# A float32 encoder trunk on one core: two matmuls of 512 and 256 columns per weight tile, in place of three of 256

## The chip, the cores and the metric

The kernel runs on one core of one Trainium2 chip. The metric is device time of one execution in microseconds, as the median of the runs. Before the change it was 1114.94 us (three runs, 1114.20 to 1115.59).

## The reference, cut to what matters

Two layers work on 256 tokens of 1024 channels in float32. All that the change touches are dense products and what follows directly on them:

```python
def swiglu(h, w_gate, w_up, w_down):              # 1024 -> 2816 -> 1024
    return (jax.nn.silu(h @ w_gate) * (h @ w_up)) @ w_down
...
x = x + 0.5 * swiglu(rmsnorm(x, g_ffa[i]), ...)   # SwiGLU a
...                                               # mixer: attention and a long convolution
y = jnp.concatenate([_rms(y_na), _rms(y_hy)], axis=-1) * g_out[i]
x = x + y @ w_out[i]                              # output projection
x = x + 0.5 * swiglu(rmsnorm(x, g_ffb[i]), ...)   # SwiGLU b
x = x + jax.nn.sigmoid(rmsnorm(x, g_ple[i]) @ w_ple_gate[i]) * (p[i] @ w_ple_proj[i])
```

After two such layers comes a last RMS norm.

## The kernel before

Activations lie with channels on the 128 partitions and the 256 tokens side by side, so a block of 128 channels is a tile of 128x256. To keep float32 accuracy on a TensorE that multiplies shorter numbers, every operand is split in two: a rounded high part and the remainder. A product of a 128x128 weight tile with a block of activations is `mm3`, three matmuls of 256 columns into one accumulator: weight high with activation high (L165), weight high with activation low (L166), weight low with activation high (L167). The two parts of an activation lie side by side in one tile of 512 columns (`xg`, `act`, `y`).

Weights stream from memory in float32. For every 8 weight tiles ScalarE (ACT) rounds them to the high part `wh` (the cast on L250, 128x1024) and VectorE (DVE) subtracts that to get the low part `wl` (L253); in the mixer every third of these subtractions goes to GpSimd (POOL). Six such halves can wait in buffers for TensorE.

What sets the order: TensorE and ACT execute in the order in which the Python code emits; DVE, POOL and SyncE execute in an order that a scheduler fixed when the program was built. Emission is paced by the products. After every third product (`TICK = 3`) a tick lets each live "fiber" (a generator of the smaller work) go one step, up to its next `yield`. An instruction that waits on DVE holds up what stands behind it on DVE.

The stages of a layer, in order: SwiGLU a (44 gate and up products of 8 weight tiles, then 8 down blocks of 22 tiles), the mixer, the output projection (8 blocks, 4 tiles of attention and 4 of convolution each), SwiGLU b as SwiGLU a, and the gated per-layer input (8 gate products of 8 tiles). The mixer's column products, scores and transforms keep `mm3` in both versions.

- In the SwiGLU a pair of gate and up shares one PSUM bank (128x512). DVE multiplies both by `rb`, the reciprocal root mean square of each token (L439; for the first two pairs L436 and L437, 256 columns each), ACT takes silu (L442), DVE multiplies silu and up (L445), ACT rounds it (L447), DVE subtracts (L449). The first four products, called heads below, run side by side over the eight input blocks `xg`, since these come one by one from the stage before.
- Normalisation is late: `Rstd` sums the squares, TensorE reduces them (L379), DVE does Newton's steps for the root (L387, L352 to L361), DVE and ACT put the result on a diagonal (L391 to L397), and TensorE spreads it (L403, L404). Squares are taken on ACT (L314) and added on POOL (L317).
- In the projection each block's two sums are multiplied by `rna` or `rhy` on DVE (L886) and added to `x`, the first on POOL, the second on DVE (both L887). When `x` of a block is final, ACT makes the high part (L329) and DVE the low part (L331) of `xg`, the next stage's input; on DVE this is one instruction.
- In the gate of the per-layer input DVE multiplies by `rb` (L985), ACT takes the sigmoid (L988), DVE multiplies (L992) and adds to `x` (L993); then follows the next stage's `xg`, or, at the very end, the transposition (L1009) and the last norm.

Of the kernel before, what the change touches and what calls it, by code (L numbers as in the profile page):

```python
# [28 lines left out]
HALF = 8  # L29

# [29 lines left out]
# columns of the packed per-partition parameters of one layer  # L60
# [15 lines left out]
def hybrid_trunk(ctx: ExitStack, tc: tile.TileContext, w, xT, pT, rpb, small, wf, zT, dft, idft, decay, out):  # L76
# [42 lines left out]
    class Fiber:  # L119
        """Work of several engines, emitted step by step between the products."""  # L120
# [39 lines left out]
    def rest(n):  # L160
        for _ in range(n):
            yield

    def mm3(o, lh, ll, rh, rl, start, stop):
        PE.matmul(o, lh, rh, start=start, stop=False)  # L165
        PE.matmul(o, lh, rl, start=False, stop=False)  # L166
        PE.matmul(o, ll, rh, start=False, stop=stop)  # L167
        if not Pace.inside:
            Pace.total += 1
            Pace.count += o.free_size() // T if hasattr(o, "free_size") else o.shape[-1] // T  # L170
            while Pace.count >= TICK:
                Pace.count -= TICK
                tick()

# [21 lines left out]
    # even times, odd times, and the latter's negative; real and imaginary parts  # L196
# [37 lines left out]
    def part(steps=1):  # L234
        """The next 8 weight tiles in their two 12-bit parts."""
        n = Stream.parted
        Stream.parted += 1
        while Stream.loaded < min(n // 2 + 2, DEPTH * PIECES):
            load()
        raw = Stream.raws[n // 2]  # L240
        h = whp.tile([P, HALF, P], F32R, tag="wh", name=nm("wh"))
        l = wlp.tile([P, HALF, P], F32R, tag="wl", name=nm("wl"))
        fb = Fiber(None)
        Stream.ready[n] = (h, l, fb)

        def go():
            k = HALF // steps
            for a in range(0, HALF, k):
                src = raw[:, n % 2 * HALF + a : n % 2 * HALF + a + k]
                S.copy(h[:, a : a + k], src)  # L250
                yield
                e = G if Stream.on_pool and n % Stream.on_pool == 0 else V
                e.tensor_sub(l[:, a : a + k], src, f(h[:, a : a + k]))  # L253
# [39 lines left out]
    class Inputs:  # L293
        """The two parts of g * x of the norm at hand."""
# [5 lines left out]
        def __getitem__(self, c):  # L300
            hl, fb = self.xs[c]
            fb.finish()
            return hl[:, :T], hl[:, T:]

    class Squares:
        """Sum of the squares of `n` blocks, in whatever order they come."""
# [27 lines left out]
    def onward(i, cg, c, before):  # L334
        """After `before`, which brings x[c] up to date, the next norm's input."""
        hl = t2(F32R, "xg")

        def go():
            yield from before
            yield  # L340
            yield from prep(i, cg, c, hl)

        scaled.append((hl, spawn(go())))

    def rsqrt(v):
        """v ** -0.5 of two columns by Newton's steps from the exponent's halving."""
# [18 lines left out]
    class Rstd:  # L365
        """1/rms of each token: `r`, tokens on partitions, and `dst`, on all partitions."""
# [58 lines left out]
    def ffn(i, cg_next, i_next):  # L425
# [5 lines left out]
        def gated(pg, pu, joint, hl):  # L431
            yield from rest(EV)
            yield from rs.wait()
            gu = t2(s="gu")
            if joint is None:
                V.tensor_mul(gu[:, :T], pg, rb)  # L436
                V.tensor_mul(gu[:, T:], pu, rb)  # L437
            else:
                V.tensor_tensor(v2(gu), v2(joint), rb2(), op=ALU.mult)  # L439
            yield  # L440
            s = t1()
            S.activation(s, gu[:, :T], AF.Silu)  # L442
            yield
            a = t1()
            V.tensor_mul(a, s, gu[:, T:])  # L445
            yield
            S.copy(hl[:, :T], a)  # L447
            yield
            V.tensor_sub(hl[:, T:], a, f(hl[:, :T]))  # L449

        def start(*a):
            hl = t2(F32R, "act")
            act.append((hl, spawn(gated(*a, hl))))

        heads = [bank()[:, :T] for _ in range(4)]
        for c in range(KD):
            xh, xl = xs[c]
            for o in heads:
                wh, wl = ws.next()
                mm3(o, wh, wl, xh, xl, c == 0, c == KD - 1)  # L460
        for j in (0, 2):
            start(heads[j], heads[j + 1], None)
        for ff in range(2, NF):
            b = bank()
            for o in (b[:, :T], b[:, T:]):
                product(o, ws, xs)
            start(None, None, b)
        ws = Tiles()
        new_norm()
        for c in range(KD):  # L470
            ps = bank()[:, :T]
            for k in range(NF):
                wh, wl = ws.next()
                hl, fb = act[k]
                fb.finish()
                mm3(ps, wh, wl, hl[:, :T], hl[:, T:], k == 0, k == NF - 1)

            def half_step(c=c, ps=ps):
                yield from rest(EV)
                V.scalar_tensor_tensor(x[c], ps, 0.5, x[c], op0=ALU.mult, op1=ALU.add)  # L480

            onward(i_next, cg_next, c, half_step())
# [8 lines left out]
    def filter_steps(i):  # L491
# [96 lines left out]
        # sums and differences of the even and the odd times' spectra  # L588
# [22 lines left out]
    def mixer(i):  # L611
# [3 lines left out]
        def columns(between=None):  # L615
            """Two blocks of 128 columns of u from the next 16 weight tiles."""
# [7 lines left out]
        # values, tokens on partitions  # L624
# [36 lines left out]
        class QK:  # L661
            """Queries and keys of a pair of heads, the queries with zeros for the other head."""
# [25 lines left out]
        class Head:  # L688
            """One head's probabilities: the scores' softmax, then turned over."""
# [56 lines left out]
        def head_norm(src, sq, ch, hl):  # L746
            """The two parts of g * y, and its squares added up."""
# [21 lines left out]
        def conv(b, chans, res):  # L769
            """Short convolution of the two blocks of channels in a bank."""  # L770
# [66 lines left out]
        def spectral(a, ps):  # L837
            """The gated input's spectrum, frequencies on partitions, times the filter's."""
# [34 lines left out]
        def project(wo, c, parts):  # L873
            ps = bank()[:, :T]
            for k in range(4):
# [3 lines left out]
                mm3(ps, wh, wl, hl[:, :T], hl[:, T:], k == 0, k == 3)  # L879
            return ps  # L880

        def add(c, ps, st, e):
            yield from rest(EV)
            yield from st.wait()
            t = t1()
            V.tensor_mul(t, ps, st.dst)  # L886
# [71 lines left out]
    def ple(i, last, given):  # L958
# [22 lines left out]
        def update(c, ps):  # L981
            yield from rest(PLE_EV)
            yield from rs.wait()
            g = t1()
            V.tensor_mul(g, ps, rb)  # L985
# [27 lines left out]
        for c in range(KD):  # L1013
            ps = bank()[:, :T]
            product(ps, ws, xs)
# [80 lines left out]
def _rpb_index():  # L1096
    """Where the bias of (token of the query, token of the key) lies; the last place outside the window."""
# [7 lines left out]
def _tiles(wm):  # L1105
    """[K, M] -> [M tiles, K tiles, 128, 128]."""
# [4 lines left out]
def _weights(a):  # L1111
# [9 lines left out]
    def swiglu(i, s):  # L1121
# [4 lines left out]
        put(_tiles(a[f"w_ff{s}_down"][i]))  # L1126
# [77 lines left out]
```

## Time and profile before

| | before |
|---|---|
| median of three runs | 1114.94 us |
| span of the profiled execution (first to last instruction) | 1112.9 us |
| granted TensorE clock, mean | 0.996 |
| PE matmuls | 8828 |
| DMA queues, share of 16 engines | 49% |

The profiled execution spans 1112.9 us, and about 2 us of the median lie around it. In the rows of a timeline the columns are start, duration, engine, line, operation, output and inputs, count; what stands in brackets is idle time before it and what ended it. A matmul's duration contains its way through the array, so the distance from one start to the next is what a matmul costs. On DVE too, back-to-back instructions overlap by some 0.08 us.

### The profile page before, as it was taken

To read this page: it belongs to the slowest core of one execution; us is meant where nothing else is said; L and a number is where in the kernel's file an instruction comes from. 1 tells how busy PE (TensorE), PEld (TensorE's weight loads), DVE (VectorE), ACT (ScalarE), POOL (GpSimd) and SP (SyncE) were. 2 spreads that over 40 slices of the span, in tenths; PEclk is the share of its full clock that TensorE was granted. 3 is DMA by queue.
4 is the path that set the end of the run, shared out by engine and by line. 5 is a ranking of instruction groups with operands and counts; after the bars stand their busy time and mean duration, and the time that the engine had idled before them with its cause. 6 is when DMAs were issued, how large, how long until landed. Compare 5 with 4: busy or idle time off the path is not lost.

```text
span 1112.9 us, 21462 instructions
## 1 busy us (share of the span) xinstructions
PE 1087.2 (98%) x8828; PEld 1074.4 (97%) x8828; DVE 840.5 (76%) x1352; ACT 600.3 (54%) x1006; POOL 205.1 (18%) x182
## 2 busy tenths in 40 slices
PE   7999999999999999999999999999999999999996
PEld 7999999999999999999999999999989999999995
DVE  4988777798999766655878878677899986665554
ACT  6555455376746444444655455544855554444444
POOL 3000111544362000011100002125433700000111
PEclk9999999999999999999999999999999999999998
DMA  8565455454335555455455554454523464555421
GB/s 319 215 236 201 154 191 186 170 173 169 114 117 197 190 189 190 176 175 183 161 195 200 215 188 174 173 185 152 190 77 114 142 217 183 189 189 186 176 95 39
DMA packets 32994, 194.29 MB, mean 175 GB/s; under 512 B 3584, under 2 KB 6528, under 8 KB 10880
## 3 DMA queue, kind: packets, MB, share of 16 engines
q1 hardware_dynamic: 32896, 192.92, 48.4%
q8 instruction: 69, 1.13, 0.4%
q14 instruction: 29, 0.24, 0.1%
HBM read 191.86 MB, written 1.05 MB: 173 GB/s over the span
## 4 chain that ended last, share of the span: by engine, by line
PE 80%; DVE 11%; ACT 4%; issue 3%; DMA 1%; POOL 1%; SPq 0%; ACTq 0%; DVEq 0%; POOLq 0%
PE ps L166 26%; PE ps L167 26%; PE ps L165 26%; DVE wl L253 2%; ACT wh L250 2%; DMA raw<-in_w 1%; DVE rt L360 1%; DVE s L783 1%; DVE s L886 1%; DVE x L887 1%; ACT t L723 1%; DVE xg L331 0%; POOL acc L317 0%; ACT t L716 0%; DVE y L752 0%
## 5 line engine op out<-in xcount | busy, mean ns | idle before, releaser
L253 DVE TENSOR_TENSOR wl<-raw,wh 128x1024 fp32r<-128x1024 f32 (+1 forms) x328 | 410.9, 1257 | 193.7 <-ACT wh L250 191.7
L250 ACT CAST wh<-raw 128x1024 fp32r<-128x1024 f32 (+1 forms) x350 | 362.0, 1040 | 321.6 <-PE ps L166 226.8
L165 PE MATMUL ps<-xg,wh 128*128 128x256 f32 x1856 | 528.2, 285 | 5.9 <-ACT xg L1032 5.9
L166 PE MATMUL ps<-xg,wh 128*128 128x256 f32 x1856 | 527.5, 284 | 5.4 <-DVE xg L331 5.3
L167 PE MATMUL ps<-xg,wl 128*128 128x256 f32 x1856 | 526.9, 284 | 0.0
L166 PEld LDWEIGHTS ps<-xg,wh 128*128 128x128 f32 x1856 | 357.7, 193 | 7.2 <-DVE xg L331 6.3
L165 PEld LDWEIGHTS ps<-xg,wh 128*128 128x128 f32 x1856 | 357.8, 193 | 6.3 <-ACT xg L1032 5.9
L167 PEld LDWEIGHTS ps<-xg,wl 128*128 128x128 f32 x1856 | 357.7, 193 | 0.0
L167 PE MATMUL ps<-act,wl 128*128 128x256 f32 x704 | 199.4, 283 | 0.0
L165 PE MATMUL ps<-act,wh 128*128 128x256 f32 x704 | 199.4, 283 | 0.0
L166 PE MATMUL ps<-act,wh 128*128 128x256 f32 x704 | 199.4, 283 | 0.0
L317 POOL TENSOR_TENSOR acc<-acc,q 128x256 f32<-128x256 f32 x62 | 65.9, 1064 | 541.2 <-ACT q L314 524.8
L165 PEld LDWEIGHTS ps<-act,wh 128*128 128x128 f32 x704 | 135.2, 192 | 0.4
L166 PEld LDWEIGHTS ps<-act,wh 128*128 128x128 f32 x704 | 135.2, 192 | 0.4
L167 PEld LDWEIGHTS ps<-act,wl 128*128 128x128 f32 x704 | 135.2, 192 | 0.0
L439 DVE TENSOR_TENSOR gu<-ps,rb 128x512 f32<-128x512 f32 x80 | 55.0, 689 | 20.6 <-PE ps L167 19.0
L253 POOL TENSOR_TENSOR wl<-raw,wh 128x1024 fp32r<-128x1024 f32 x22 | 55.0, 2499 | 62.7 <-ACT wh L250 49.9
L566 POOL TENSOR_TENSOR t<-t,t 128x512 f32<-128x512 f32 x4 | 5.7, 1414 | 225.7 <-PE ps L167 121.0
L329 ACT ACTIVATE xg<-x,sm 128x256 fp32r<-128x256 f32 x56 | 28.1, 506 | 33.2 <-DVE x L480 14.0
L397 ACT ACTIVATE s<-ident,rl 128x128 fp32r<-128x128 f32 x24 | 8.3, 395 | 65.4 <-DVE rl L392 65.4
L442 ACT ACTIVATE s<-gu 128x256 f32<-128x256 f32 x88 | 35.9, 414 | 12.8 <-DVE gu L439 12.0
L449 DVE TENSOR_TENSOR act<-s,act 128x256 fp32r<-128x256 f32 x88 | 38.3, 444 | 0.0
(193 smaller groups left out, 1222.7 us busy)
## 6 DMA issues: line engine op xcount, KB each, us to landing
raw<-in_w SPq DMA_DIRECT2D x172, 1024.0 KB, 4.8
bias<-in_rpb SPq DMA_DIRECT2D x16, 256.0 KB, 2.8
raw<-in_w SPq DMA_DIRECT2D x4, 256.0 KB, 4.6
x<-in_xT SPq DMA_DIRECT2D x8, 128.0 KB, 4.8
raw<-in_w SPq DMA_DIRECT2D x2, 512.0 KB, 5.7
t<-in_wf SPq DMA_DIRECT2D x4, 256.0 KB, 5.4
dec<-in_decay SPq DMA_DIRECT2D x4, 256.0 KB, 5.4
out<-o SPq DMA_DIRECT2D x4, 256.0 KB, 2.4
```

The lines of the kernel that those rows point to most:

```text
L165: PE.matmul(o, lh, rh, start=start, stop=False)
L166: PE.matmul(o, lh, rl, start=False, stop=False)
L167: PE.matmul(o, ll, rh, start=False, stop=stop)
L250: S.copy(h[:, a : a + k], src)
L253: e.tensor_sub(l[:, a : a + k], src, f(h[:, a : a + k]))
L317: G.tensor_add(self.ac, self.ac, q)
L329: S.activation(hl[:, :T], x[c], AF.Copy, scale=g)
L360: V.tensor_scalar(r[:, c], y[:, c], y[:, c], hv[:, c], op0=ALU.mult, op1=ALU.mult)
L439: V.tensor_tensor(v2(gu), v2(joint), rb2(), op=ALU.mult)
L442: S.activation(s, gu[:, :T], AF.Silu)
L449: V.tensor_sub(hl[:, T:], a, f(hl[:, :T]))
L723: S.activation(e[:, cs], e[:, cs], AF.Copy, scale=ri[:, tt : tt + 1])
```

## The change

Four places take a new way for the product of a weight tile: gate, up and down of both SwiGLUs, the output projection, and the gate of the per-layer input. The high weight part multiplies both activation parts in one matmul of 512 columns over a whole PSUM bank (L191). The matmul of the low weight part with the high activation part (256 columns, into the second half of the bank, L200) is put on a list, which is emitted when it holds eight or a product ends. The bank then holds two halves that must be added. `summed` does it: ACT copies the second half to SBUF, and two ticks later DVE adds the first half (L208). The multiplication by `rb` follows as an operation of its own in place: gate's on DVE (L489), up's on POOL (L490). The down blocks add their halves to `x` with two operations instead of one (L529). Gate and up have a bank each. Last, the first two of the eight down blocks are done in two parts: 16 tiles of block 0, 16 of block 1, then 6 of each; the weights are packed in that order. Lines move: 250 to 285, 253 to 288, 331 to 370, 360 and 361 to 399 and 400, 396 to 435, 403 to 442, 445 to 497, 449 to 502, 886 and 887 to 945 and 946.

```diff
+    class Wide:
+        later = []
+        @classmethod
+        def mm(cls, b, lh, ll, r, start, stop):
+            PE.matmul(b, lh, r, start=start, stop=False)
+            cls.later.append((b[:, T:], ll, r[:, :T], stop))
+            if stop or len(cls.later) == GROUP:
+                cls.flush()
+            paced()
+        @classmethod
+        def flush(cls):
+            for o, ll, rh, stop in cls.later:
+                PE.matmul(o, ll, rh, start=False, stop=stop)
+            cls.later.clear()
+    def summed(dst, b):
+        S.copy(dst, b[:, T:])
+        yield
+        yield
+        V.tensor_add(dst, dst, b[:, :T])
...
-        def gated(pg, pu, joint, hl):
+        def gated(gate, up, hl):
...
-                V.tensor_tensor(v2(gu), v2(joint), rb2(), op=ALU.mult)
+            V.tensor_mul(g, g, rb)
+            G.tensor_mul(u, u, rb)
...
         def add(c, ps, st, e):
             yield from rest(EV)
+            t = t1()
+            yield from summed(t, ps)
             yield from st.wait()
-            t = t1()
-            V.tensor_mul(t, ps, st.dst)
+            V.tensor_mul(t, t, st.dst)
             e.tensor_add(x[c], x[c], t)
...
         def update(c, ps):
             yield from rest(PLE_EV)
+            g = t1()
+            yield from summed(g, ps)
             yield from rs.wait()
-            g = t1()
-            V.tensor_mul(g, ps, rb)
+            V.tensor_mul(g, g, rb)
...
-                V.scalar_tensor_tensor(x[c], ps, 0.5, x[c], op0=ALU.mult, op1=ALU.add)
+            for b in (ps[:, :T], ps[:, T:]):
+                V.scalar_tensor_tensor(x[c], b, 0.5, x[c], op0=ALU.mult, op1=ALU.add)
...
+DOWN = [(c, k) for ks in (range(16), range(16, NF)) for c in range(2) for k in ks]
+DOWN += [(c, k) for c in range(2, KD) for k in range(NF)]
```

TensorE at the third pair of the first SwiGLU (the first product after the heads; `xg_141` to `xg_148` are the eight input blocks, `wh_181` and `wl_182` the two parts of eight weight tiles), before:

```order
L165 MATMUL ps_333<-xg_141,wh_181 128x256 [waits Activation_49]
L166 MATMUL ps_333<-xg_141,wh_181 128x256
L167 MATMUL ps_333<-xg_141,wl_182 128x256 [waits DVE_49]
L165 MATMUL ps_333<-xg_142,wh_181 128x256
L166 MATMUL ps_333<-xg_142,wh_181 128x256
L167 MATMUL ps_333<-xg_142,wl_182 128x256
```

and now:

```order
L191 MATMUL ps_305<-xg_141,wh_181 128x512 [waits Activation_49]
L191 MATMUL ps_305<-xg_142,wh_181 128x512
L191 MATMUL ps_305<-xg_143,wh_181 128x512
...
L191 MATMUL ps_305<-xg_148,wh_181 128x512
L200 MATMUL ps_305<-xg_141,wl_182 128x256 [waits DVE_49]
L200 MATMUL ps_305<-xg_142,wl_182 128x256
```

Eight wide matmuls stand in a row, then eight narrow ones; the low weight part is first asked for eight matmuls after the high part.

DVE at the end of the mixer of layer 0, where the projection's sums are taken up (`ps` are accumulators of the attention's half, `rna` its normalisation), before:

```order
L752 SCALAR_TENSOR_TENSOR y_3996<-s_4021,sm,y_3996 128x256 [waits Activation_49]
L886 TENSOR_TENSOR s_4086<-ps_4045,rna_2756 128x256 [waits Activation_49]
L886 TENSOR_TENSOR s_4089<-ps_4017,rna_2756 128x256
L886 TENSOR_TENSOR s_4092<-ps_3997,rna_2756 128x256
L886 TENSOR_TENSOR s_4105<-ps_4062,rna_2756 128x256 [waits PE_49]
L253 TENSOR_TENSOR wl_4082<-raw_3700,wh_4081 128x1024 [waits DMAHW2_49,Activation_49]
L886 TENSOR_TENSOR s_4133<-ps_4080,rna_2756 128x256 [waits PE_49]
```

and now:

```order
L810 SCALAR_TENSOR_TENSOR y_3604<-s_3623,sm,y_3604 128x256 [waits Activation_49]
L208 TENSOR_TENSOR s_3640<-s_3640,ps_3605 128x256 [waits PE_49]
L208 TENSOR_TENSOR s_3663<-s_3663,ps_3621 128x256 [waits Activation_49]
L945 TENSOR_TENSOR s_3640<-s_3640,rna_2364 128x256 [waits DVE_49,Activation_49]
L945 TENSOR_TENSOR s_3663<-s_3663,rna_2364 128x256 [waits DVE_49]
L208 TENSOR_TENSOR s_3681<-s_3681,ps_3647 128x256 [waits PE_49,Activation_49]
L288 TENSOR_TENSOR wl_3679<-raw_3308,wh_3678 128x1024 [waits DMAHW2_49,PE_49,Activation_49]
L945 TENSOR_TENSOR s_3681<-s_3681,rna_2364 128x256 [waits DVE_49]
```

Each of the sixteen multiplications of the stage has an addition ahead of it, most of which wait for ACT's copy.

DVE in the first norm of the program, where Newton's steps for the root run between the splits of the first weights (`rt` are the steps' values, `gu` the heads' sums), before:

```order
L354 TENSOR_SCALAR rt_398<-rt_397 128x2 [waits DVE_49]
L253 TENSOR_TENSOR wl_304<-raw_178,wh_303 128x1024 [waits DMAHW1_49,Activation_49]
L253 TENSOR_TENSOR wl_335<-raw_178,wh_334 128x1024 [waits Activation_49]
L253 TENSOR_TENSOR wl_365<-raw_215,wh_364 128x1024 [waits DMAHW4_49,Activation_49]
L360 TENSOR_SCALAR rt_403<-rt_398,rt_399 128x1 [waits DVE_49]
```

and now:

```order
L393 TENSOR_SCALAR rt_365<-rt_364 128x2 [waits DVE_49]
L288 TENSOR_TENSOR wl_280<-raw_178,wh_279 128x1024 [waits DMAHW1_49,Activation_49]
L288 TENSOR_TENSOR wl_307<-raw_178,wh_306 128x1024 [waits Activation_49]
L208 TENSOR_TENSOR gu_302<-gu_302,ps_188 128x256 [waits Activation_49]
L208 TENSOR_TENSOR gu_301<-gu_301,ps_187 128x256 [waits Activation_49]
L208 TENSOR_TENSOR gu_300<-gu_300,ps_186 128x256 [waits Activation_49]
L208 TENSOR_TENSOR gu_299<-gu_299,ps_185 128x256 [waits Activation_49]
L288 TENSOR_TENSOR wl_335<-raw_203,wh_334 128x1024 [waits DMAHW4_49,Activation_49]
L399 TENSOR_SCALAR rt_370<-rt_365,rt_366 128x1 [waits DVE_49]
```

The four heads' additions stand ahead of the first Newton step (a fifth, of the next product, stands behind it), since they no longer wait for the norm.

More of the change, by code (lines that the diff above doesn't have):

```diff
@@ L29 @@
 HALF = 8
+GROUP = 8
 E = mybir.EngineType
@@ L167, in mm3, with paced @@
         PE.matmul(o, ll, rh, start=False, stop=stop)
+        paced(o.free_size() // T if hasattr(o, "free_size") else o.shape[-1] // T)
+    def paced(n=1):
         if not Pace.inside:
             Pace.total += 1
-            Pace.count += o.free_size() // T if hasattr(o, "free_size") else o.shape[-1] // T
+            Pace.count += n
             while Pace.count >= TICK:
@@ L300, in __getitem__, with both @@
         def __getitem__(self, c):
+            hl = self.both(c)
+            return hl[:, :T], hl[:, T:]
+        def both(self, c):
             hl, fb = self.xs[c]
             fb.finish()
-            return hl[:, :T], hl[:, T:]
+            return hl
     class Squares:
@@ L422, in product, with product2 @@
             mm3(o, wh, wl, xh, xl, c == 0, c == KD - 1)
+    def product2(b, ws, xs):
+        for c in range(KD):
+            wh, wl = ws.next()
+            Wide.mm(b, wh, wl, xs.both(c), c == 0, c == KD - 1)
     def ffn(i, cg_next, i_next):
@@ L429, in ffn, with taken, go @@
         rs = norm(xs, STAT0 if Stream.used == 0 else STAT_F)
-        def gated(pg, pu, joint, hl):
-            yield from rest(EV)
-            yield from rs.wait()
[L434 to L439, printed above, removed]
+        def taken(b):
+            dst = t1(s="gu")
+            def go():
+                yield from rest(EV)
+                yield from summed(dst, b)
+            return dst, spawn(go())
@@ L440, in gated @@
+        def gated(gate, up, hl):
+            (g, gf), (u, uf) = gate, up
+            while not (gf.done and uf.done):
+                yield
+            yield from rs.wait()
+            V.tensor_mul(g, g, rb)
+            G.tensor_mul(u, u, rb)
+            yield
             yield
             s = t1()
-            S.activation(s, gu[:, :T], AF.Silu)
+            S.activation(s, g, AF.Silu)
             yield
-            a = t1()
-            V.tensor_mul(a, s, gu[:, T:])
             yield
-            S.copy(hl[:, :T], a)
+            V.tensor_mul(s, s, u)
@@ L448, in gated, with start @@
             yield
-            V.tensor_sub(hl[:, T:], a, f(hl[:, :T]))
-        def start(*a):
+            yield
+            S.copy(hl[:, :T], s)
+            yield
+            V.tensor_sub(hl[:, T:], s, f(hl[:, :T]))
+        def start(gate, up):
             hl = t2(F32R, "act")
-            act.append((hl, spawn(gated(*a, hl))))
-        heads = [bank()[:, :T] for _ in range(4)]
+            act.append((hl, spawn(gated(gate, up, hl))))
+        heads = [bank() for _ in range(4)]
         for c in range(KD):
-            xh, xl = xs[c]
-            for o in heads:
+            for b in heads:
@@ L459, in ffn @@
                 wh, wl = ws.next()
-                mm3(o, wh, wl, xh, xl, c == 0, c == KD - 1)
-        for j in (0, 2):
-            start(heads[j], heads[j + 1], None)
+                Wide.mm(b, wh, wl, xs.both(c), c == 0, c == KD - 1)
+        heads = [taken(b) for b in heads]
+        start(*heads[:2])
+        start(*heads[2:])
         for ff in range(2, NF):
[L464 to L467, printed above, removed]
+            pair = []
+            for _ in range(2):
+                b = bank()
+                product2(b, ws, xs)
+                pair.append(taken(b))
+            start(*pair)
@@ L468, in ffn, with half_step @@
         ws = Tiles()
         new_norm()
[L470 to L479, printed above, removed]
-                V.scalar_tensor_tensor(x[c], ps, 0.5, x[c], op0=ALU.mult, op1=ALU.add)
-            onward(i_next, cg_next, c, half_step())
+        def half_step(c, ps):
+            yield from rest(EV)
+            for b in (ps[:, :T], ps[:, T:]):
+                V.scalar_tensor_tensor(x[c], b, 0.5, x[c], op0=ALU.mult, op1=ALU.add)
@@ L484, in stacked @@
+        out = {}
+        for c, k in DOWN:
+            if k == 0:
+                out[c] = bank()
+            wh, wl = ws.next()
+            hl, fb = act[k]
+            fb.finish()
+            Wide.mm(out[c], wh, wl, hl, k == 0, k == NF - 1)
+            if k == NF - 1:
+                onward(i_next, cg_next, c, half_step(c, out.pop(c)))
     def stacked(src, h):
@@ L1013, in ple @@
         for c in range(KD):
-            ps = bank()[:, :T]
-            product(ps, ws, xs)
+            ps = bank()
+            product2(ps, ws, xs)
             if last:
```

6 lines of the change are left out of this document (3 added, 3 removed).

## The prediction

> **What bounds the kernel now.** I read the page first, its busy times and the chain that ended last:
>
> ```profile
> PE 1087.2 (98%) x8828; PEld 1074.4 (97%) x8828; DVE 840.5 (76%) x1352; ACT 600.3 (54%) x1006; POOL 205.1 (18%) x182
> PE 80%; DVE 11%; ACT 4%; issue 3%; DMA 1%; POOL 1%; SPq 0%; ACTq 0%; DVEq 0%; POOLq 0%
> PE ps L166 26%; PE ps L167 26%; PE ps L165 26%; DVE wl L253 2%; ACT wh L250 2%; DMA raw<-in_w 1%; DVE rt L360 1%; DVE s L783 1%; DVE s L886 1%; DVE x L887 1%; ACT t L723 1%; DVE xg L331 0%; POOL acc L317 0%; ACT t L716 0%; DVE y L752 0%
> ```
>
> TensorE has work 98% of the time and three matmul lines make up 78% of the chain. But DVE holds 11% of the chain, so next I asked for busy time by stage (columns: busy us and count of PE, PEld, DVE, ACT, POOL, then clock, DMA share, GB/s) and for TensorE's waits:
>
> ```profile
> 5.90:140.00 134.10, 133.15 (x1075) 132.30 (x1076) 108.09 (x178) 74.69 (x121) 11.44 (x10) 1.00 0.63 229
> 306.50:330.50 24.00, 24.00 (x203) 24.00 (x201) 22.72 (x60) 10.92 (x21) 16.01 (x13) 1.00 0.28 95
> 330.50:344.00 13.50, 10.58 (x84) 9.97 (x83) 13.50 (x20) 10.58 (x21) 9.27 (x8) 1.00 0.52 181
> 344.00:461.60 117.60, 117.60 (x983) 117.60 (x982) 83.56 (x126) 57.41 (x87) 0.00 (x0) 1.00 0.53 193
> 553.70:564.00 10.30, 10.30 (x88) 10.30 (x87) 9.94 (x17) 7.73 (x15) 3.12 (x4) 1.00 0.68 237
> 564.00:684.00 120.00, 120.00 (x996) 119.64 (x995) 95.94 (x158) 61.45 (x97) 3.62 (x3) 1.00 0.53 188
> 851.00:875.60 24.60, 24.60 (x207) 24.60 (x206) 23.56 (x60) 11.57 (x21) 15.38 (x13) 1.00 0.29 100
> PE ps L166 <- DVE xg L331: 5.3, 5, 1.3
> ```
>
> In SwiGLU b (344 to 461.6) DVE is busy 71%: TensorE alone is the limit. In the output projection (306.5 to 330.5, again at 851) and the heads after it (to 344) DVE is busy 36.2 of 37.5 us, and TensorE waits there for DVE's `xg`. Into SwiGLU a of layer 1 (553.7 to 564) DVE is full too. So the change takes time from TensorE everywhere and adds to DVE everywhere, and the two count in different stages.
>
> **What TensorE saves.** Starts of matmuls, 256 columns, then 512, then the change between them:
>
> ```profile
> 218.90 0.28 PE L165 MATMUL ps<-xg,wh 128*128 128x256 f32 x1
> 219.98 0.28 PE L165 MATMUL ps<-xg,wh 128*128 128x256 f32 x1
> 752.70 0.39 PE L165 MATMUL ps<-wh,xg 128*128 128x512 f32 x1
> 757.91 0.39 PE L167 MATMUL ps<-wh,xg 128*128 128x512 f32 x1
> 273.35 0.40 PE L165 MATMUL ps<-t,dft_h 128*128 128x512 f32 x1
> 276.10 0.28 PE L165 MATMUL ps<-s,t 128*128 128x256 f32 x1
> 277.53 0.40 PE L165 MATMUL ps<-t,dft_h 128*128 128x512 f32 x1
> ```
>
> Nine steps of 256 columns in 1.08 us are 120 ns each; 23 steps of 512 in 5.21 us are 226.5 ns. A weight tile falls from 360 to 346.5 ns, 13.5 ns less. Changing width costs: twelve wide ones right after narrow ones take 2.75 us (32 ns over 12 x 226.5), the twelve narrow ones after them 1.43 us (10 ns less). A group of eight changes width once each way: 8 x 13.5 - 32 + 10 = 86 ns, so 10.75 ns a tile. I take that; the ends are 13.5 (the change costs nothing) and 8 (it costs twice those 22 ns).
>
> The tiles: 528 in each of four SwiGLUs, 128 in the projections, 128 in the gates, 2368. Where TensorE is paced by others its saving is lost: both projections with the heads behind them (2 x 96), the gate before 553.7 and the heads after it (96), and 69 tiles up to the first statistics, which wait for POOL (27.41 below). Left are 2011 x 10.75 ns = **21.6 us**.
>
> The Trainium skill, TensorE: Matmul & The Clock Gate, "Back-to-back issue gap", gives a warm isolated gap of N/2.4 + 2.5 ns: 109 at 256 columns, 216 at 512. By it a tile would save 2.5 ns, 2011 tiles about 5 us (an estimate from that page). The rows show 11 ns over it at both widths, so a matmul fewer is worth more here.
>
> **What the output projection gives back.** DVE's groups there (306.3 to 343.7) and the distance between back-to-back starts:
>
> ```profile
> L253 DVE TENSOR_TENSOR wl<-raw,wh 128x1024 fp32r<-128x1024 f32 x7 | 10.4, 1486 | 0.7 <-ACT wh L250 0.7
> L887 DVE TENSOR_TENSOR x<-x,s 128x256 f32<-128x256 f32 x8 | 7.8, 1004 | 0.0
> L886 DVE TENSOR_TENSOR s<-ps,rhy 128x256 f32<-128x256 f32 x8 | 3.1, 411 | 0.0
> 545.32 1.22 DVE L253 TENSOR_TENSOR wl<-raw,wh 128x1024 fp32r<-128x1024 f32 x1
> 546.45 0.42 DVE L993 TENSOR_TENSOR x<-x,s 128x256 f32<-128x256 f32 x1
> 546.79 0.87 DVE L331 SCALAR_TENSOR_TENSOR xg<-x,sm,xg 128x256 fp32r<-128x256 f32 x2
> ```
>
> An operation of 256 columns costs DVE 0.34 us, a split 1.13. The projection gets 16 additions (L208), 5.4 us. By its new order DVE also does seven splits up to the last `xg`, where six ended there before: 1.1 us. Idle in the stretch is 1.28 us; I let half of it take some. That is 5.4 + 1.1 - 0.6 = 5.9 us a layer, and every bit reaches TensorE, since the heads need each `xg` as it comes: **-11.8 us** for both. Ends: 4 (all idle used, the split fits) to 6.5 a layer. The 16 copies on ACT, which is busy 10.9 of 24 us, are covered by its idle time; without that, see the second rival.
>
> **Into SwiGLU a of layer 1.** The last `xg` there:
>
> ```profile
> 562.68 0.96 DVE L331 SCALAR_TENSOR_TENSOR xg<-x,sm,xg 128x256 fp32r<-128x256 f32 x1
> 563.78 0.28 PE L165 MATMUL ps<-xg,wh 128*128 128x256 f32 x1
> ```
>
> It is ready at 563.64, and TensorE takes it at 563.78: 0.14 us to spare, 0.36 idle on DVE. Added are 8 additions (2.7) and one split more ahead of it (1.1): 3.9 - 0.5, **-3.4 us**, ends 0 and 4.5.
>
> **The start.** POOL sets when the first statistics run; then Newton's steps must reach L403 in time:
>
> ```profile
> 27.41 0.61 PE L379 MATMUL ps<-onesf,acc 128*128 128x1 f32 x4 [0.80 <-POOL acc L317]
> 34.47 0.69 ACT L397 ACTIVATE s<-ident,rl 128x128 fp32r<-128x128 f32 x2 [6.29 <-DVE rl L392]
> 35.52 0.28 PE L403 MATMUL ps<-s,ones 128*128 128x256 f32 x1
> ```
>
> The diagonal was ready at 35.16, 0.36 before its use. Five additions stand in the chain now, 1.7 us, and TensorE comes 0.2 earlier: **-1.5 us**; everything behind L403 on TensorE waits too. Ends 0 and 2.5.
>
> **The tail.** In the last gate block a copy and an addition precede the sigmoid:
>
> ```profile
> 1099.95 0.42 DVE L985 TENSOR_TENSOR s<-ps,rb 128x256 f32<-128x256 f32 x1 [0.96 <-PE ps L167]
> L405 ACT COPY rb<-ps 128x256 f32<-128x256 f32 x1 | 0.4, 372 | 1.5 <-PE ps L404 1.5
> ```
>
> 0.37 + 0.42, **-0.8 us**.
>
> **What costs nothing.** A pair of gate and up gave DVE one product of 512 columns and two of 256, and now five of 256. Rows of SwiGLU b (350 to 460), and POOL's nearest to the product by `rb`:
>
> ```profile
> L439 DVE TENSOR_TENSOR gu<-ps,rb 128x512 f32<-128x512 f32 x19 | 13.1, 691 | 5.5 <-PE ps L167 5.1 <-ACT rb L405 0.5
> L445 DVE TENSOR_TENSOR s<-s,gu 128x256 f32<-128x256 f32 x21 | 8.6, 418 | 0.0
> L887 POOL TENSOR_TENSOR x<-x,s 128x256 f32<-128x256 f32 x16 | 15.2, 982 | 2.4 <-DVE s L886 2.4
> ```
>
> Five of 0.42 against 0.69 + 0.84 are 0.57 more a pair, 12.5 us a SwiGLU: 96 of SwiGLU b's 114. SwiGLU a carries the filter's work as well: layer 1 goes from 95.9 of 120 to 108.4 of 116.2. POOL's product meets DVE's: where both add `x` in the projection, DVE takes 1.00 us (L887) against 0.41 with an accumulator as input (L886), 0.59 a meeting. If two pairs in three meet, 8.6 us, DVE comes to 117.0 of 116.2. The six buffered halves hold 48 tiles, 17 us of TensorE's work, so I take 0; without that cover it is 0.8 us, and 5.2 if every pair meets. ACT gains two copies of 0.37 a pair (61.5 to 78 of 116): hidden. The down blocks' second `scalar_tensor_tensor` is 0.34 us for every 22 tiles (7.6 us), hidden behind the next block. Splitting the first two down blocks puts off the last `act` from the 22nd tile to the 37th, while its chain grew by the two copies and the yields; five operations of half a microsecond with their ticks fit into 12.5 us: nothing, at worst 2 us a SwiGLU.
>
> **Sum.** 21.6 - 11.8 - 3.4 - 1.5 - 0.8 = 4.1 us less: a span of 1108.8. Some 2.0 us lie around a span (1114.9 against 1112.9), so **1110.8 us**. The unknowns alone (8 to 13.5 ns, 4 to 6.5 us a projection, the three ends of the rest) reach from 1097 to 1120 if all fall on one side; from 1101 to 1119 I call the forecast's own range.
>
> **The rivals.**
> - *DVE's additions are covered.* For it: sums of the attention half can be added before its norm is known. Against it: `xg` is waited for in five places already, with DVE idle 1.28 us. It leaves 2299 tiles x 10.75 = 24.7, less 0.8 and 0.5: 1091.5. Some cover would give 1095 to 1103. Chance 0.20.
> - *DVE waits for ACT in the projection (slower).* DVE executes in a fixed order, and each L208 needs ACT's copy, which may stand behind a cast of 1.05 us. Half a cast and the copy are 0.9 us, during which all of DVE stands, `xg` too. Against it: DVE waits for ACT only 0.7 us in this stretch now, and copies are emitted two ticks ahead. Five such waits a layer and one at 553.7 take 9.9 us: 1120.7. From seven in all on the kernel is slower than before by over 0.2%. Chance 0.26.
> - *Wide matmuls stay slow between narrow ones (slower).* After the statistics' small matmuls, 15 wide ones take 3.55 us:
>
> ```profile
> 215.00 0.49 PE L165 MATMUL ps<-wh,xg 128*128 128x512 f32 x1
> 218.55 0.28 PE L165 MATMUL ps<-xg,wh 128*128 128x256 f32 x1
> ```
>
>  That is 237 ns each; a tile would save 3 ns, 6.0 us in all, and the time would be 1114.9 + 17.5 - 6.0 = 1126. The runs at 273.35 and 752.70 speak against it. The Trainium skill's formula, above, would end near there. Chance 0.06.
>
> **How the numbers follow.** The forecast has 0.48. About 0.2% (2.2 us) is what a measurement can tell from no change here; the forecast lies 4 below the median, so of its 0.48, 0.32 fall below 1112.7, 0.11 within and 0.05 above. With the rivals: faster 0.32 + 0.20 = 0.52; same 0.11 + 0.04 of the ACT case = 0.15; slower 0.05 + 0.22 + 0.06 = 0.33. The range for 8 in 10 takes in the forecast's ends, most of the first rival's partial cover and the second rival: 1095 to 1122.
>
> **What would show it.** Right: groups of L191 at about 229 ns and L200 at 119; SwiGLU b's gate and up 3 to 4 us shorter; DVE without a gap from the projection's first L208 to the last L370, and that stretch near 43 us; larger waits of L191 for `xg`; L442 waiting some 1.5 us. Wrong: idle times of DVE ahead of L208 ended by ACT's copy (second rival), waits of TensorE for `wl` in the SwiGLUs (the cover is gone), projections no longer than before (first rival), or L191 at 235 ns (third).

## The result, and the profile after

The changed kernel takes 1126.30 us (median of four runs, 1125.94 to 1126.73), the kernel before 1114.57 in the same series: a ratio of 1.0101, 95% interval 1.0087 to 1.0116. It is slower by 1.0%, where the forecast was 1110.8 us, faster, with a range of 1095 to 1122. The profiled execution spans 1124.2 us, against 1112.9.

The page of the changed kernel, its busy times, the granted clock in 40 slices of the span, and the chain that ended last:

```profile
PE 1077.0 (96%) x6460; PEld 955.9 (85%) x6460; DVE 918.1 (82%) x1600; ACT 659.9 (59%) x1230; POOL 303.8 (27%) x270
PEclk9999999999998999999989999999999899999997
PE 76%; DVE 15%; ACT 4%; issue 3%; DMA 1%; POOL 0%; SPq 0%; ACTq 0%; DVEq 0%; POOLq 0%
```

TensorE is busy 10 us less and the span is 11 us longer. DVE's part of the chain grew from 11 to 15%. Three slices in the middle show a lower clock, where before all but the last stood at 9. By stage the changed kernel gives (columns as in the prediction: the length, then busy us and count by engine, and the clock behind POOL's count):

```profile
139.01:204.16 65.15, 65.15 (x372) 57.17 (x371) 54.57 (x64) 34.85 (x51) 16.16 (x13) 1.00 0.51 171
204.16:304.70 100.54, 99.03 (x747) 94.30 (x746) 86.00 (x150) 65.27 (x136) 42.20 (x38) 1.00 0.48 161
304.70:334.68 29.98, 24.84 (x140) 21.09 (x139) 28.01 (x69) 13.63 (x31) 15.49 (x13) 1.00 0.31 105
334.68:465.24 130.56, 127.09 (x708) 110.53 (x709) 108.61 (x193) 81.72 (x156) 28.74 (x29) 0.97 0.55 186
532.49:689.38 156.89, 152.30 (x861) 133.35 (x860) 139.80 (x264) 98.04 (x188) 30.95 (x30) 0.98 0.52 181
```

and the same five stages before:

```profile
140.04:207.06 67.02, 67.02 (x547) 66.36 (x546) 47.83 (x53) 34.89 (x50) 11.54 (x10) 1.00 0.52 187
207.06:306.43 99.37, 98.63 (x748) 94.24 (x747) 88.03 (x150) 64.98 (x136) 42.84 (x38) 1.00 0.43 153
306.43:330.39 23.96, 23.96 (x203) 23.96 (x202) 22.65 (x61) 10.88 (x21) 16.01 (x13) 1.00 0.27 93
330.39:461.48 131.09, 128.17 (x1065) 127.56 (x1064) 97.17 (x146) 68.10 (x107) 9.27 (x8) 1.00 0.53 191
530.60:684.22 153.62, 153.62 (x1277) 153.26 (x1276) 125.05 (x217) 83.92 (x137) 10.71 (x10) 1.00 0.52 186
```

In this order they are the down blocks of SwiGLU a, the mixer, the output projection, the heads with gate and up of SwiGLU b (all of layer 0), and the gate with SwiGLU a of layer 1. The down blocks got 1.87 us shorter, which is 176 tiles by 10.6 ns. The mixer, which keeps its products, got 1.2 us longer. The projection got 6.0 us longer, though it issues 64 matmuls fewer. SwiGLU b, with 352 tiles, won 0.5 us in place of 3.8, and the stage of the gate lost 3.3.

TensorE's waits, after:

```profile
PE ps L191 <- DVE xg L370: 13.1, 10, 3.3
PE ps L442 <- DVE s L435: 7.0, 4, 2.9
PE ps L191 <- DVE s L208: 3.8, 4, 1.7
```

These three lines grew most, and all are for DVE: for `xg` (5.3 us before), for the diagonals that spread the norms and for banks that an addition still has to read (no such waits before).

In the projection and the heads (304.7 to 351) the groups of DVE show what fills it:

```profile
L945 DVE TENSOR_TENSOR s<-s,rna 128x256 f32<-128x256 f32 x8 | 8.1, 1031 | 0.0
L208 DVE TENSOR_TENSOR s<-s,ps 128x256 f32<-128x256 f32 x16 | 6.1, 408 | 0.0
L946 DVE TENSOR_TENSOR x<-x,s 128x256 f32<-128x256 f32 x8 | 5.3, 687 | 0.0
L945 DVE TENSOR_TENSOR s<-s,rhy 128x256 f32<-128x256 f32 x8 | 3.8, 494 | 0.0
```

The 16 additions take 0.41 us each, as priced. But the 16 multiplications, which took 2.9 (`rna`) and 3.1 us (`rhy`) by L886, take 8.1 and 3.8. Against that, the additions to `x` fell from 7.8 to 5.3 us, and the splits from 10.4 to 8.9. Two rows of the timelines of DVE and POOL show where the long multiplications come from:

```profile
313.47 2.29 DVE L945 TENSOR_TENSOR s<-s,rna 128x256 f32<-128x256 f32 x2
312.57 2.58 POOL L288 TENSOR_TENSOR wl<-raw,wh 128x1024 fp32r<-128x1024 f32 x1
```

The first of the two multiplications lasts until 315.42, just past the end of POOL's split (315.15); the second takes 0.41 us again. L886 read one input from the accumulator; L945 reads both from SBUF, as POOL's split does. Over both layers ten of L945's 32 multiplications have nothing on POOL beside them, and each takes 0.41 or 0.42 us; all 13 that take over 0.5 us overlap work on POOL.

### The profile page after: what moved, and what is told of

The parts are those of the page before. It is cut to its first block, busy times and chain, and to the rows that moved or that the text cites. A ratio compares the mean times of both kernels' runs of the same rounds, so it can differ in the third digit from the quotient of the medians.

```text
span 1124.2 us, 17666 instructions
## 1 busy us (share of the span) xinstructions
PE 1077.0 (96%) x6460; PEld 955.9 (85%) x6460; DVE 918.1 (82%) x1600; ACT 659.9 (59%) x1230; POOL 303.8 (27%) x270
## 4 chain that ended last, share of the span: by engine, by line
PE 76%; DVE 15%; ACT 4%; issue 3%; DMA 1%; POOL 0%; SPq 0%; ACTq 0%; DVEq 0%; POOLq 0%
PE ps L191 43%; PE ps L200 22%; DVE wl L288 3%; PE ps L171 3%; PE ps L172 3%; PE ps L170 3%; ACT wh L285 2%; DVE s L945 2%; DMA raw<-in_w 1%; DVE xg L370 1%; DVE s L208 1%; DVE rt L399 1%; DVE s L841 1%; ACT t L781 1%; DVE x L946 1%
## 5 line engine op out<-in xcount | busy, mean ns | idle before, releaser
L191 PE MATMUL ps<-xg,wh 128*128 128x512 f32 x1536 | 401.1, 399 | 22.6 <-DVE xg L370 13.1
L191 PEld LDWEIGHTS ps<-xg,wh 128*128 128x128 f32 x1536 | 278.9, 192 | 76.8 <-DVE xg L370 13.6
L200 PEld LDWEIGHTS ps<-xg,wl 128*128 128x128 f32 x1536 | 213.8, 193 | 15.3
L200 PE MATMUL ps<-xg,wl 128*128 128x256 f32 x1536 | 219.4, 285 | 0.0
L490 POOL TENSOR_TENSOR gu<-gu,rb 128x256 f32<-128x256 f32 x88 | 95.0, 1084 | 368.4 <-DVE gu L208 323.6
L191 PE MATMUL ps<-act,wh 128*128 128x512 f32 x704 | 179.0, 392 | 0.0
L191 PEld LDWEIGHTS ps<-act,wh 128*128 128x128 f32 x704 | 126.2, 189 | 22.1
L200 PEld LDWEIGHTS ps<-act,wl 128*128 128x128 f32 x704 | 97.1, 190 | 7.6
L200 PE MATMUL ps<-act,wl 128*128 128x256 f32 x704 | 99.4, 282 | 0.0
L170 PE MATMUL ps<-xg,wh 128*128 128x256 f32 x320 | 90.8, 284 | 0.0
L171 PE MATMUL ps<-xg,wh 128*128 128x256 f32 x320 | 90.5, 283 | 0.0
L172 PE MATMUL ps<-xg,wl 128*128 128x256 f32 x320 | 90.5, 283 | 0.0
L208 DVE TENSOR_TENSOR gu<-gu,ps 128x256 f32<-128x256 f32 x176 | 71.3, 411 | 0.1
L170 PEld LDWEIGHTS ps<-xg,wh 128*128 128x128 f32 x320 | 61.4, 192 | 0.1
L171 PEld LDWEIGHTS ps<-xg,wh 128*128 128x128 f32 x320 | 61.4, 192 | 0.1
L172 PEld LDWEIGHTS ps<-xg,wl 128*128 128x128 f32 x320 | 61.4, 192 | 0.0
```

What stands on the lines that cost most here:

```text
L191: PE.matmul(b, lh, r, start=start, stop=False)
L208: V.tensor_add(dst, dst, b[:, :T])
L490: G.tensor_mul(u, u, rb)
```

## The experiments

Nine kernels were run. Theory A: the loss arises where `xg` is handed over while DVE is full, from additions, multiplications that now meet POOL, and a halved TensorE clock behind its waits. Theory B: DVE's extra work in the SwiGLUs themselves eats the lead of the weights. Where ratios are given they are against the kernel before in the same series.

**e1_proj_mm3.** The projection as before the change:

```diff
-                Wide.mm(ps, wh, wl, hl, k == 0, k == 3)
+                mm3(ps, wh, wl, hl[:, :T], hl[:, T:], k == 0, k == 3)
...
-            yield from summed(t, ps)
             yield from st.wait()
-            V.tensor_mul(t, t, st.dst)
+            V.tensor_mul(t, ps, st.dst)
```

> The output projection goes back to three matmuls of 256 columns and one sum; all else as in the changed kernel. Theory A (the loss arises where each xg is handed over while DVE is full: additions, multiplications that now meet POOL, and the halved clock after TensorE's waits): projection, heads and SwiGLU b of a layer took 155.1 and 154.3 us before and take 160.5 and 161.1 now; they should take 151 to 152, so 18 to 19 us go and the time is 1107 to 1109. Theory B (the extra DVE work in the SwiGLUs themselves eats the lead of the weights, and the projection only shows it): only the 16 additions a layer go, 10.8 us, so 1115 to 1117, and TensorE still waits over 5 us a layer for xg.

1106.80 us, ratio 0.9924 (0.9905 to 0.9943). From the projection to SwiGLU b's last up product the two layers take 151.7 and 151.3 us, so 8.9 and 9.9 are gone. Theory A gave 1107 to 1109, theory B 1115 to 1117.

**e2_gate_mm3.** The gate of the per-layer input as before the change:

```diff
-            yield from summed(g, ps)
             yield from rs.wait()
-            V.tensor_mul(g, g, rb)
+            V.tensor_mul(g, ps, rb)
...
-            product2(ps, ws, xs)
+            product(ps, ws, xs)
```

> The gate of the per-layer input goes back to three matmuls and one sum; all else as in the changed kernel. Theory A: from the gate of layer 0 to the end of the next gate and up products it took 153.6 us before, 156.9 now and should take 150 to 151; from the last gate to the end 38.1 before, 40.1 now, 38 again: 8 to 9 us less, 1117 to 1118. Theory B: only 8 additions in front of SwiGLU a and the two in the tail go, 3.5 us, so 1122 to 1123.

1118.67 us, ratio 1.0029 (1.0017 to 1.0040). The stretch from the gate to SwiGLU a's last up product takes 150.0 us, 6.9 less; from the last gate's first matmul to the end it is 38.9 in place of 39.7 (37.9 before; the expectation's 38.1 and 40.1 start 0.1 and 0.35 ahead of that matmul). A again, but for the tail, where 1.0 of the 1.8 us stays.

**e3_swiglu_only.** Both edits together.

> Both go back, so that only the SwiGLUs keep two matmuls per weight tile. Theory A: the two gains add up, 1098 to 1101, which is faster than before by 1.2 to 1.5%; what is left of TensorE's saving is 2112 tiles by 10.9 ns less the start. Theory B: 1111 to 1114, no better than before, with TensorE waiting for xg at the heads more than before.

1099.82 us, ratio 0.9862 (0.9845 to 0.9879): 15 us faster than before and 26 faster than the changed kernel. DVE is as busy as in the changed kernel, 82%:

```profile
PE 1068.6 (97%) x6716; PEld 964.6 (88%) x6716; DVE 897.0 (82%) x1552; ACT 647.3 (59%) x1182; POOL 305.1 (28%) x270
524.74:674.76 150.02, 150.02 (x925) 134.69 (x924) 136.44 (x257) 95.78 (x179) 29.70 (x30) 1.00 0.55 189
```

The second row is the stage of the gate and SwiGLU a of layer 1: TensorE works without a break, though DVE is busy 91% of it. The gains of e1 and e2, taken singly, come to 27 us together, so they add up, and theory B has fallen.

**e4_psum_sum.** In the projection the sum goes back into the accumulator, and the multiplication reads it there:

```diff
-            yield from summed(t, ps)
+            S.copy(t, ps[:, T:])
+            yield
+            yield
+            V.tensor_add(ps[:, :T], t, ps[:, :T])
             yield from st.wait()
-            V.tensor_mul(t, t, st.dst)
+            V.tensor_mul(t, ps[:, :T], st.dst)
```

> In the projection alone, DVE writes the sum of the two halves back into the accumulator and multiplies from there by rna or rhy, instead of from SBUF: as many operations, but the multiplication has one SBUF input in place of two. If DVE's multiplications are slow because they meet POOL (L945 takes 1.01 us with rna and 0.60 with rhy, where L886 from the accumulator took 0.41), they fall to 0.41 each, some of the meetings move on to the additions of x, and 4 to 10 us go: 1116 to 1122. If it is the number of operations and their waits alone, nothing changes: 1125.5 to 1127.

1116.76 us, ratio 1.0013 (1.0004 to 1.0022). With as many operations, and as many columns in each, the kernel is 9.5 us faster. DVE in projection and heads (304 to 347):

```profile
L946 DVE TENSOR_TENSOR ps<-s,ps 128x256 f32<-128x256 f32 x16 | 6.2, 416 | 0.0
L949 DVE TENSOR_TENSOR x<-x,s 128x256 f32<-128x256 f32 x8 | 6.2, 791 | 0.0
L948 DVE TENSOR_TENSOR s<-ps,rna 128x256 f32<-128x256 f32 x8 | 3.1, 413 | 0.0
L948 DVE TENSOR_TENSOR s<-ps,rhy 128x256 f32<-128x256 f32 x8 | 3.1, 410 | 0.0
```

Every multiplication (L948) is back at 0.41 us, though 24 of the 32 have POOL at work beside them; L949, which adds two inputs from SBUF, is longer than in the changed kernel (0.79 in place of 0.69). So the meetings with POOL are shown, and what this edit saves of them is some four tenths of the projection's loss: 3.3 and 4.9 us of the two layers' stretches, which is what DVE gets shorter by from the projection's first addition to the last `xg` (38.3 to 35.0 and 38.5 to 33.6 us). Another 2.5 us went in the stage of the gate, which the edit doesn't touch: there the clock, halved in the changed kernel's profiled execution, stayed up in this one, behind the same wait (3.32 us).

**e5_up_on_dve.** `G.tensor_mul(u, u, rb)` becomes `V.tensor_mul(u, u, rb)`.

> The changed kernel, with the product of up and rb on DVE in place of POOL. Theory A: the SwiGLUs' middle is paced by TensorE and the buffered weights cover DVE there, so SwiGLU b (from the heads' end) keeps its time; DVE has 0.34 us more per pair and loses the meetings with POOL (L489 0.54 and L502 0.48 us come down to 0.42): 1125 to 1130. Theory B (POOL's products are what hurts DVE in the SwiGLUs): 1116 to 1123.

1126.48 us, ratio 1.0100 (1.0085 to 1.0115), the same as the changed kernel. POOL's 88 products meet DVE's in the SwiGLUs (L489 has a mean of 0.54 us there), but moving them to DVE changes nothing.

**e6_down_in_order.** `DOWN = [(c, k) for c in range(KD) for k in range(NF)]`: the down blocks one after the other.

> The changed kernel, with the down blocks in their plain order again (22 tiles of block 0, then 22 of block 1). My prediction said the last act is ready 10 to 12.5 us after the last up product. In plain order it is needed after 21 tiles of 0.349 us, 7.3 us, so TensorE would wait 2.5 to 5 us in each of four SwiGLUs: 1136 to 1146. If the chain behind the last product is shorter than 7 us, the order of the down blocks is worth nothing: 1125 to 1127.5.

1142.08 us, ratio 1.0241 (1.0226 to 1.0257), 16 us slower than the changed kernel. TensorE's waits gain a line:

```profile
PE ps L190 <- DVE act L501: 10.9, 4, 3.9
150.00:157.00 7.00, 7.00 (x28) 5.96 (x28) 3.51 (x6) 2.71 (x5) 0.00 (x0) 0.64 0.26 107
```

Four waits for the last `act`, 2.7 us on average, are 11 of the 16 us. In the first SwiGLU this `act` comes 10.7 us after the down blocks begin (138.84 to 149.56); the prediction had said that its chain fits into 12.5. The second row, of the stages, is the stretch behind the first of these waits: the clock is 0.64 there, which may account for the other 5 us. The new order of the down blocks is worth 16 us with the longer chain.

**e7_group1.** e3_swiglu_only with `GROUP = 1`.

> Only the SwiGLUs with two matmuls per tile (e3_swiglu_only), and groups of one instead of eight: 512, 256, 512, 256 columns. If what a change of width costs adds up (22 ns for each wide-and-narrow change, by the rows of before), a tile takes 346.5 + 22 in place of 349.1 ns: 2112 x 19 ns, 40 us more, 1135 to 1142. If the price shrinks in short runs, as the changed kernel's few alternating tiles at its start suggest (353 ns a tile), it is 2112 x 4 ns: 1106 to 1112. If only the columns count: 1098 to 1102.

1103.37 us, ratio 0.9894 (0.9879 to 0.9909). In SwiGLU b of layer 0 the tiles follow each other like this:

```profile
400.44 0.40 PE L191 MATMUL ps<-xg,wh 128*128 128x512 f32 x1
403.97 0.40 PE L191 MATMUL ps<-xg,wh 128*128 128x512 f32 x1
```

They are ten tiles apart: 353 ns a tile, where groups of eight take 349. So the price of a change of width does not add up. By their ratios 3.6 us separate the two groupings, whose intervals touch at 0.9879; the middle expectation was right in kind and 3 us too high. Where those 3 us came from was not followed up.

**e8_narrow_heads.** e3_swiglu_only, with the four heads of each SwiGLU by `mm3` into half a bank, and both multiplications by `rb` from there on DVE:

```diff
-                Wide.mm(b, wh, wl, xs.both(c), c == 0, c == KD - 1)
+                mm3(b, wh, wl, xh, xl, c == 0, c == KD - 1)
...
+                g, u = t1(s="gu"), t1(s="gu")
+                V.tensor_mul(g, gate, rb)
+                V.tensor_mul(u, up, rb)
```

> Only the SwiGLUs with two matmuls per tile (e3_swiglu_only), and in them the four heads, which follow right on the handing over of xg, with three matmuls and one sum again. Theory A: the four additions a SwiGLU leave the places where DVE is full (1.4 us behind each projection, 1.5 us at the start), against 128 tiles by 10.9 ns that are no longer saved: 2 to 5 us less than e3_swiglu_only, 1095 to 1098. If the additions at the heads are covered there, 1.4 us more: 1100 to 1102.

1101.35 us, ratio 0.9880 (0.9864 to 0.9897), which can't be told from e3_swiglu_only (0.9845 to 0.9879). The gain of 2 to 5 us didn't come; the time fits the other expectation, that the additions at the heads are covered in that kernel.

**e9_keep_busy.** The changed kernel, with matmuls that nobody reads in TensorE's longest wait:

```diff
+            if i == 1 and cg_next == C_MIX and c == KD - 1:
+                spare = bank()
+                for k in range(13):
+                    PE.matmul(spare, ones, xs.both(0), start=True, stop=True)
```

> The changed kernel, with 13 matmuls of 512 columns into a spare bank ahead of the last input block's four head products in SwiGLU a of layer 1; nothing reads them. There TensorE waits 3.3 us for the last xg, and the 15 matmuls that follow run at half the clock (426 ns at 512 columns, 212 at 256), 2.1 us over their usual pace. If the halved clock follows from the wait and costs by itself, the filled wait (13 x 0.23 us = 3.0 us) keeps the clock up, the matmuls behind run at 229 and 119 ns, and the stretch from the gate of layer 0 to SwiGLU a's last gate and up product falls from 156.9 us by about 2: 1124 to 1125. If the clock is set by something else, or DVE sets the pace behind as well, the stretch keeps its time or grows: 1126 to 1128.

1123.85 us, ratio 1.0068 (1.0052 to 1.0085), and the stretch takes 154.4 us in place of 156.9. TensorE's timeline in the changed kernel and then in this one, in both from the last `xg` on:

```profile
570.25 0.79 PE L191 MATMUL ps<-xg,wh 128*128 128x512 f32 x1 [3.31 <-DVE xg L370]
570.84 1.27 PE L200 MATMUL ps<-xg,wl 128*128 128x256 f32 x5
571.91 0.63 PE L191 MATMUL ps<-xg,wh 128*128 128x512 f32 x1
572.33 0.41 PE L200 MATMUL ps<-xg,wl 128*128 128x256 f32 x1
```

```profile
566.67 3.11 PE L513 MATMUL ps<-xg,ones 128*128 128x512 f32 x13
570.20 0.50 PE L191 MATMUL ps<-xg,wh 128*128 128x512 f32 x1 [0.42 <-DVE xg L370]
570.54 0.76 PE L200 MATMUL ps<-xg,wl 128*128 128x256 f32 x5
571.14 0.40 PE L191 MATMUL ps<-xg,wh 128*128 128x512 f32 x1
```

The next wide matmul after the first of these comes 1.66 us later in the one and 0.94 in the other. Between 570.25 and 574.50 the granted clock was 0.50 in the changed kernel and 1.00 here. So this wait was paid twice: as it lasted, and by the slow matmuls behind it.

The wait alone doesn't decide it, though. The profiled executions of five kernels have the same wait there, 3.31 to 3.35 us. In the changed kernel the clock was halved for 5.6 us of TensorE's work behind it (570.25 to 575.80), in e1 for 3.4, in e4 not at all, and the stage took 156.9, 155.9 and 154.4 us, which is about what half the clock costs over those times. Each kernel has one profile only, so that the filled wait kept the clock up in e9 is likely, not certain; the times of its four runs (1123.10 to 1124.71) do lie clear of the changed kernel's.

## Why the prediction was wrong

**What TensorE saves** was right. Groups of eight in SwiGLU b of the changed kernel:

```profile
415.31 2.00 PE L191 MATMUL ps<-xg,wh 128*128 128x512 f32 x8
418.10 2.00 PE L191 MATMUL ps<-xg,wh 128*128 128x512 f32 x8
```

2.79 us for eight tiles are 349 ns a tile, 11 ns less than 360, against 10.75 forecast. So the third rival (wide matmuls stay slow) fell, with its 3 ns a tile, and so did the 2.5 ns by the formula of the Trainium skill (TensorE: Matmul & The Clock Gate, "Back-to-back issue gap"). That the rival's time, 1126, is the one measured is chance.

**What the output projection gives back** is the step that failed: a term mis-sized, with a mechanism missing. I put it at 5.9 us a layer. With 320 tiles behind the heads that do save 3.5 us, the stretches of 155.0 to 160.5 and 154.3 to 161.1 us cost 9.0 and 10.4; undoing it gave 8.9 and 9.9. DVE's rows, from the projection's first addition or multiplication to the last `xg`, say where this comes from. That stretch of DVE grew from 29.4 to 38.3 us in layer 0 and from 28.6 to 38.5 in layer 1 (us, from start to start):

| | forecast | layer 0 | layer 1 |
|---|---|---|---|
| additions of the halves | +5.4 | +5.3 | +5.4 |
| multiplications by `rna`, `rhy` | 0 | +5.7 | +7.0 |
| additions to `x` | 0 | -2.5 | -4.6 |
| splits, one more than before | +1.1 | -0.4 | +0.6 |
| idle | -0.6 | +0.6 | +1.6 |
| the rest | 0 | +0.3 | -0.1 |
| whole | +5.9 | +8.9 | +9.9 |

The additions were as reckoned. What I priced wrongly are first the multiplications: I let each stay at L886's price, although the change takes their input from the accumulator to SBUF. The rows needed stood in the prediction itself (1.00 us with two SBUF inputs against 0.41 with one); I used them for POOL's new product in the SwiGLUs and not here. A good part of it comes back, since the additions to `x` meet POOL less often (5 of 16 overlap its work, 9 before), and the split more costs little because the other splits got shorter. Second, I let DVE's idle time shrink, and it grew:

```profile
324.94 1.23 DVE L288 TENSOR_TENSOR wl<-raw,wh 128x1024 fp32r<-128x1024 f32 x1 [1.36 <-ACT wh L285]
```

The Trainium skill, SBUF — State Buffer, "Who interferes with whom", says that a DVE instruction with two SBUF inputs contends with a GpSimd instruction that reads SBUF, and that one with at most one SBUF input, outside the modes that use two ports, doesn't; e4 agrees (0.41 us each).

**Into SwiGLU a of layer 1** I put 3.4 us; it cost 6.9 (e2). TensorE, which had no wait there before, waits 1.28 and 3.31 us for `xg`, 4.6 in place of 3.4. Some 2.5 us came on top by the halved clock (e4, e9), a cost that no step of mine had. The prediction's column of the clock gave no hint of it: it was 1.00 in all rows, and TensorE's waits for `xg` were 1.3 us at most. The Trainium skill, TensorE: Matmul & The Clock Gate, "HAM oscillation", has the clock fall in gaps of more than about 3.4 us. The traces agree with that only in part: 3.31 us lies just under it, e4 has the same wait at a full clock, and from 334.7 to 349.8 in the changed kernel the mean clock was 0.77 with no wait over 2.1 us.

**The start** was right: from its first matmul on, the stage of SwiGLU a in layer 0 lost 1.6 us to it, 1.5 forecast (the 69 tiles that I left out there reach to the spreading of the norm at 35.52, not to the statistics at 27.41):

```profile
36.54 0.35 PE L442 MATMUL ps<-s,ones 128*128 128x256 f32 x1 [1.54 <-DVE s L435]
```

**The tail** cost 2.5 us (37.9 to 39.7, with 0.7 saved), 0.8 forecast. Undoing the gate gives back 0.8 and loses the 0.7 saved, so 1.5 of it is the gate's new form; the other 1.0 stays without it and wasn't tested.

**What costs nothing** held: the four stretches of down blocks got shorter by 1.9 us each, TensorE never waited for weights in SwiGLU a, and POOL's product costs no more than one on DVE would (e5). That the longer chain into the down blocks would be hidden held because of their new order (e6).

The mixer's 1.2 us in layer 0 and 1.0 in layer 1 were in no step. In layer 0 about 0.5 us of it lie where the norm is spread (L442), and 0.6 where the scores wait for ACT:

```profile
PE ps L170 <- ACT t L740: 0.8, 2, 0.6
```

e3_swiglu_only has the mixer at 100.5 us as well, so neither projection nor gate is to blame. Why ACT and the norm come later there was not tested and stays open.

The differences add up: 7.6 us for both projections, 3.4 for the gate's stage (by its length before and after), 2.1 for the mixer, 1.7 for the tail, 0.1 at the start and 0.7 because the first matmul started at 6.59 in place of 5.92 are 15.6, less 0.3 for tiles that saved 10.9 in place of 10.75 ns. With the forecast's span of 1108.8 that is 1124.1, and 1124.2 was measured. The start of the first matmul lies between 5.7 and 7.3 us in the ten profiles of changed kernels, so I put it down to chance.

**The rivals.** The first (additions covered) fell in the projection and the gate. The second (DVE waits for ACT) gave a nearer time, 1120.7, in the main for a wrong reason:

```profile
DVE s L208 <- ACT s L205: 3.5, 4, 1.4
```

Over the whole run DVE waited for ACT's copies four times, and in the projection it had no idle time ahead of an addition or a multiplication. It did wait for ACT's casts, ahead of a split, and once for ACT's part of an `xg`: idle time in the stretch of the table went from 0.7 to 1.4 and from 0.4 to 1.9 us. So the sign that I had named, DVE without a gap from L208 to the last L370, failed as well; from the norm's first step (304.78) to the last `xg` (351.10) layer 0 takes 46.3 us, where I had 43.

## What to carry to other kernels

When an edit moves an operand from the accumulator to SBUF, price the instruction anew by a row with the same places of its inputs: beside a busy POOL the same multiplication cost 0.41 us with one input in the accumulator and 1.03 on average with both in SBUF, and writing the sum back into the accumulator undid that. Apply a saving on the engine that bounds most stages only to the stages that it bounds: two matmuls per tile were worth 15 us in the SwiGLUs and cost 26 in projection and gate, where DVE hands over the next input. Reckon with slow matmuls behind a TensorE wait of some microseconds: here they cost 0 to 2.5 us behind one of 3.3.

## What the runs showed of the hardware

That a change of width costs little even when every matmul changes it was new to me: 353 ns for 512 and 256 columns in turn, against 349 in groups of eight and 346.5 by the two steady paces. And behind one and the same TensorE wait of 3.3 us the granted clock was halved for 5.6 us in one profile, for 3.4 in another and not at all in a third; with the wait filled by matmuls without any use it stayed at 1.00.
